# Projection weights and mixes in a scan: loads placed apart from their casts

## The chip, the cores and the metric

The kernel runs on one core of one Trainium2 chip. The metric is the time of one execution in device microseconds (us), as the median of the runs. The profile comes from one further execution on the same core, and its engines are called PE (TensorE: matmuls; PEld its weight loads), DVE (VectorE), ACT (ScalarE), POOL (GpSimd) and SP (SyncE, whose queue issues most of the DMAs here).

## What is computed

One step of a hybrid backbone with one layer. 128 context tokens and 2048 latent tokens of width 1024 pass an RMS norm, one input projection, two groups of heads, one output projection, a gated residual and a last RMS norm.

```python
def _layer(x, mod, s0, is_latent, lp):
    shift, scale, gate = jnp.split(mod, 3, axis=-1)
    h = _rmsnorm(x, lp['norm_g']) * (1.0 + scale) + shift
    proj = h @ lp['w_in']
    r, k, v, g_a, b_gate, c_gate, u_conv, g_b = jnp.split(proj, IN_SPLITS, axis=-1)
    rkv = _token_shift(jnp.concatenate([r, k, v], axis=-1), lp['shift_mu'].reshape(-1), is_latent)
    ya, s_final = _wkv(h, r, k, v, s0, lp)
    ya = ya.astype(x.dtype) * jax.nn.silu(g_a)
    yb = b_gate * _short_conv(c_gate * u_conv, lp['conv_w'], is_latent) * jax.nn.silu(g_b)
    u = jnp.concatenate([ya, yb], axis=-1) @ lp['w_out']
    return x + gate * u, s_final
```

`_wkv` is a delta-rule state update, token after token, run in both directions over eight heads of 64. Head group A (the "attention" half, 512 channels) comes from it; head group B (the "conv" half, 512 channels) comes from a short convolution and needs no scan.

## The kernel before, in words

Phase 1 (up to about 1004 us) computes the input projection, the gates and the conv half, and stores the operands of the scan and the mixed activations to scratch in HBM: `mixT` holds, for each token, the 1024 channels that enter the output projection. The conv channels of `mixT` are complete when phase 1 ends; the attention channels come out of the scan, an output block at a time.

Phase 2 is the scan, in NST = 17 stages. A round plays a string of letters (`ROUND`, `ROUND_FILL`, `ROUND_MORE`, `ROUND_END`, `ROUND_LAST`, lines 750 to 754). The loop in `main` runs round s for stage s: `L` (psF, psG), `U` and `u` (psU, psW) and `B` (psX, psE) prepare stage s+1 with matmuls, `b` is what was left of the stage's own preparation, `S` is one of the state steps (matmul psS, then DVE's `sv` on L1163), `f` and `T` finish an output block of the stages before (`finish`), and `a` is one piece of filling work from the output projection: three matmuls into psa (L1419 to L1421). Every fp32 operand is split into a high and a low half, so a product is three matmuls: high by high, high by low, low by high.

The order of PE in the scan is written out by these strings: `mm`, `tr` and `pin` chain each matmul behind the one before (`behind`, `O.last`). `now` ties another instruction behind the last matmul. What is not tied is placed by the scheduler; the order on each engine's queue is then fixed. SP issues DMAs in that order.

The output projection's weights `wout` are 1024 by 1024. Rows 512 to 1023 (k = 4 to 7, the conv half) are loaded in the first three rounds by `conv_weights` (`woraw`, L1398), cast to the high half by ACT (`split`, L1386) and reduced to the low half by DVE (L1387). Rows 0 to 511 are loaded, cast and reduced in the last rounds by `att_weights` (L1444, low half by POOL). The activations of a tile of 128 tokens are loaded by `load_mix` (L1403): `mxc` is the conv half and becomes `mhc`, `mxa` the attention half and becomes `mha`.

`fill` multiplies the conv half ahead, for the nine tiles of AHEAD: eight pieces (psa) a tile, stored as z0. In the middle rounds (`ROUND_FILL`) three pieces stand one by one, so a tile's mix is loaded every second or third round, in the same call that casts it.

POOL inverts the small triangular blocks of the stages (`solve_steps`, L951 to L971) with the scratch tiles `zt`, `ztmp` and `ab`; `partI(s + 7)` starts it seven stages ahead, with `ab` loaded on SP's queue (L941). The result goes to scratch (L971) and comes back as `zc` (L1043) when stage s+1 is prepared.

`finish(p, blk, y)` turns a block of scan outputs into attention channels of `mixT`: it loads the gate `sg` (L1201), squares y into `w` (ACT), reduces it, scales y (L1218), loads q into a second `w`, transposes with psT (L863), multiplies by gate and weight into `yo` (L1231), adds q (L1233) and stores `yo` to `mixT` (L1237). The tiles `sg`, `w` and `yo` have one buffer each.

PSUM has eight banks: in the scan `ps_tile` (L829) draws the pools p2 (three banks) and pm (one, every fourth call), psS has three and psa one.

Phase 3, the tail, finishes the projection tile by tile (psu, the order of TILES): the attention half, with the conv half too where it was not done ahead, then gate, residual, norm and store.

Of the kernel before, what the change touches and what calls it, by code (L numbers as in the profile page):

```python
# [745 lines left out]
NST = 17  # L746
# [11 lines left out]
def phase2(K):  # L758
# [45 lines left out]
    def setup_rest():  # L804
# [54 lines left out]
    def now(r):  # L859
        behind(r, O.last)  # L860
# [327 lines left out]
    def finish(p, blk, y):  # L1188

        t0 = NCTX + 512 * blk if blk is not None else 0  # L1190
        sg = tl([128, 512], "sg", 1)
# [18 lines left out]
        w = tl([128, 4, 128], "w", 1)  # L1210
        P.activation(w[:], y[:], AF.Square)
        yield
        ss = tl([128, 8], "yss", 2)
        V.tensor_reduce(ss[:], heads(w[:]), mybir.AxisListType.X, ALU.add)
# [4 lines left out]
        q = tl([128, 512], "w", 1)  # L1219
# [9 lines left out]
        o = tl([128, 512], "yo", 1)  # L1229
# [40 lines left out]
    def main():  # L1270
# [13 lines left out]
        tail = fill = iter(())  # L1284
        conv = K.conv_weights()
        for s in range(NST):
# [6 lines left out]
            for _ in range(3 if s < 3 else 0):  # L1293
                next(conv, None)
            if s == 2:
                fill = K.fill()
                next(fill)
            if NST - 4 < s < NST - 1:
                K.att_weights(s - NST + 3)
            gens = dict(L=W, b=own, u=uu, U=uu, B=bb, S=partS(s, st, sts.get(s + 1)))  # L1300

            def play(tokens):
                for c in tokens:
# [4 lines left out]
                    elif c == "T":  # L1308
                        for f in todo:
                            run(f)  # L1310
                    elif c == "a":
                        next(fill, None)
                    else:
                        next(gens[c])
                        if c == "S":
                            next(tail, None)

            if more:
                play(ROUND if s < 3 else ROUND_FILL if s < NST - 4 else ROUND_MORE if s < NST - 2 else ROUND_END)
            else:  # L1320
                for k in (2, 3):
                    K.att_weights(k)
                play(ROUND_LAST)
# [7 lines left out]
                run(fill)  # L1331
# [8 lines left out]
        for p in (O.pS, O.p2):  # L1340
            p.close()
        K.rest(tail)
        O.pf.close()
# [3 lines left out]
    K.early, K.main, K.spare, K.ahead1, K.fill_tile, K.pin, K.now = early, main, spare, ahead1, fill_tile, pin, now  # L1347
# [25 lines left out]
def phase3(K):  # L1373
# [8 lines left out]
    wk = {}  # L1382

    def split(hi, lo, raw, copy, eng):

        copy(hi, raw)  # L1386
        eng.tensor_tensor(lo, raw, hi.bitcast(F32), ALU.subtract)  # L1387
# [4 lines left out]
    def conv_weights():  # L1392
        for k in CONV:
            t = [O.r.tile([128, 1024], F32R, name=f"wo{x}{k}") for x in "hl"]
            wk[k] = [[x[:, c] for c in HALF] for x in t]
            for n, c in enumerate(HALF):
                raw = O.r.tile([128, 512], F32, tag="raw", name=f"woraw{k}", bufs=1)
                K.now(D(raw[:], A["wout"][k * 128:(k + 1) * 128, c]))  # L1398
                split(wk[k][0][n], wk[k][1][n], raw[:], P.copy, V)
                yield  # L1400

    def load_mix(raw, i, ks):
        K.now(D(raw.rearrange("p (k t) -> p k t", t=128), S["mixT"].rearrange("(k p) t -> p k t", p=128)[:, ks[0]:ks[0] + 4, i * 128:i * 128 + 128]))  # L1403

    def conv_mix(i):

        raw = O.r.tile([128, 512], F32, tag="raw", name=f"mxc{i}", bufs=1)
        load_mix(raw[:], i, CONV)
        t = O.r.tile([128, 1024], F32R, tag="mhc", name=f"mhc{i}", bufs=2)
        m = [t[:, c] for c in HALF]  # L1410
        split(*m, raw[:], P.copy, V)
        return m

    def product(ps, m, ks, h, n, start, stop, pin=lambda r: None):
# [4 lines left out]
        pin(T.matmul(ps[:], hi[:, c], wh, start=start and n == 0, stop=False))  # L1419
        pin(T.matmul(ps[:], hi[:, c], wl, start=False, stop=False))  # L1420
        pin(T.matmul(ps[:], lo[:, c], wh, start=False, stop=stop and n == 3))  # L1421

    def fill():

        nxt = conv_mix(AHEAD[0])
        yield
        for x, i in enumerate(AHEAD):
            m = nxt
            for h in range(2):
                ps = K.fill_tile(f"psa{i}_{h}")  # L1430
                for n in range(4):
                    product(ps, m, CONV, h, n, True, True, K.pin)
                    if n == 0 and h and x + 1 < len(AHEAD):
                        nxt = conv_mix(AHEAD[x + 1])
# [6 lines left out]
    def att_weights(k):  # L1441

        raw = K.spare(f"woraw{k}", F32, ("ab", "ab2")[k % 2])
        K.now(D(raw[:], A["wout"][k * 128:(k + 1) * 128, :]))  # L1444
        if k == 3:
            wk[k] = [[K.spare(f"wo{x}3{c}", F32R, "F", 512)[:] for c in range(2)] for x in "hl"]
        else:
            t = [K.spare(f"wo{x}{k}", F32R, f"o{(2, 0, 1)[k]}{n}") for n, x in enumerate("hl")]
            wk[k] = [[x[:, c] for c in HALF] for x in t]
        for n, c in enumerate(HALF):  # L1450
            split(wk[k][0][n], wk[k][1][n], raw[:, c], P.copy, G)

    def tail():
        O.pr = Pool(K, "p3pr", "right", 1, PSUM)
# [7 lines left out]
        for s in range(2):  # L1462
            D(gb[:, s], S["gate"][s:s + 1, :].broadcast_to((128, 1024)))
        fg = tl([128, 1024], "fg", "", b=1)
        D(fg[:], A["fg"].broadcast_to((128, 1024)))
        eps = tl([128, 1], "eps3", "", b=1)
        V.memset(eps[:], 1e-6)
        yield

        for i in TILES:  # L1470
            t0 = i * 128
            mc = None if i in AHEAD else conv_mix(i)
            assert K.mixed[(i - 1) // 4 if i else None] == (4 if i else 1)
            raw = K.spare(f"mxa{i}", F32, "zt", 512)
            load_mix(raw[:], i, ATT)
            t = tl([128, 1024], "mha", i, F32R)
            ma = [t[:, c] for c in HALF]
            split(*ma, raw[:], P.copy, V)
            if not mc:
                z0 = tl([128, 1024], "z0", i)  # L1480
                D(z0[:], S["z0"][i])
            xt = tl([128, 1024], "x3", i)
            D(xt[:], A["x"][t0:t0 + 128, :])
# [3 lines left out]
            last = i == TILES[-1]  # L1487
            for n, cs in enumerate(HALF):
                ps = O.pu.tile([128, 512], F32, tag="u", name=f"psu{i}_{n}")
                if mc:  # L1490
                    for k in range(4):
                        product(ps, mc, CONV, n, k, True, False)
                for k in range(4):
                    product(ps, ma, ATT, n, k, not mc, True)
                if mc:
                    V.tensor_tensor(z[:, cs], ps[:], gb[:, s, cs], ALU.mult)
                else:
                    V.tensor_tensor(z[:, cs], ps[:], z0[:, cs], ALU.add)
# [19 lines left out]
    K.weights, K.conv_weights, K.fill, K.att_weights, K.tail, K.rest = weights, conv_weights, fill, att_weights, tail, rest  # L1518
# [45 lines left out]
```

## Time and profile before

| | us |
|---|---|
| median of 3 runs | 1682.65 |
| lowest, highest | 1678.48, 6477.67 |
| the profiled execution | 1678.87 |
| its span, first to last instruction | 1677.1 |
| mean granted TensorE clock | 0.965 of full speed |

An engine's busy time is the sum of its instructions; register, semaphore and DMA-issuing instructions are not in it. A row of the timeline has its start, its length, the engine, the line, what is written and read, how many were put together, and in brackets the idle time just before and what ended it. A row for SP (SPq) is the issue of a DMA, not its transfer. The windows view gives busy times and the clock that the throttle granted to PE for chosen stretches. The waits view gives, for each engine, the total, the number and the longest of the idle times by what ended them. A wait for several things is put down to the last one.

### The profile page before, as it was taken

The numbers are of one execution on the slowest core, as the hardware profiler recorded it, in microseconds if no ns is written. First come the engines' busy times: TensorE is split into PE (matmuls) and PEld (weight loads), VectorE is DVE, ScalarE is ACT, GpSimd is POOL, SyncE is SP. The second block draws the span as 40 slices with busy tenths as digits, with TensorE's granted clock in tenths as the row PEclk, the third lists the DMA queues.
The fourth block names the chain that finished last, engine by engine and source line by source line (L and its number), as shares of the span: only waits on it lengthen the run. The fifth ranks groups of instructions, "written<-read, shape, count | busy, mean of one in ns | idle before, by whom it ended". The sixth has DMA issues, their size and how long they took to land.

```text
span 1677.1 us, 42417 instructions
## 1 busy us (share of the span) xinstructions
PE 1545.4 (92%) x17160; PEld 1402.0 (84%) x17160; DVE 1123.9 (67%) x2246; ACT 778.4 (46%) x1645; POOL 575.4 (34%) x1030
## 2 busy tenths in 40 slices
PE   5899999999999999999999996898889898887998
PEld 2799998999999999999899895777777787665886
DVE  5876877884648775568786964575566665556664
ACT  4544565553426344255443114656556565542332
POOL 0011221110112111012863656687887800101431
PEclk8999999999999999999999998799899899999999
DMA  9677767665646565656758576566575654427652
GB/s 378 202 259 242 252 240 257 221 217 203 219 136 200 210 191 180 219 177 205 244 190 281 199 228 184 148 184 167 156 221 162 174 152 146 114 84 257 232 200 101
DMA packets 242451, 336.67 MB, mean 201 GB/s; under 512 B 91784, under 2 KB 192392, under 8 KB 228176
## 3 DMA queue, kind: packets, MB, share of 16 engines
q1 hardware_dynamic: 233712, 323.27, 60.1%
q10 hardware_dynamic: 7344, 6.76, 1.3%
q0 software_dynamic: 1200, 3.93, 0.6%
q8 instruction: 135, 2.21, 0.6%
q14 instruction: 60, 0.49, 0.1%
HBM read 212.64 MB, written 121.26 MB: 199 GB/s over the span
## 4 chain that ended last, share of the span: by engine, by line
PE 44%; DVE 9%; POOL 7%; DMA 7%; ACT 4%; issue 3%; SPq 1%; DVEq 0%; ACTq 0%; POOLq 0%
PE psE L849 3%; POOL zt L966 3%; PE psu L1419 3%; PE psu L1421 3%; PE psu L1420 3%; DMA mxc<-scr_mixT 2%; POOL ztmp L963 2%; PE psS L849 2%; DMA woraw<-in_wout 1%; ACT fg L838 1%; PE mmc L166 1%; PE mmg L168 1%; PE mmg L166 1%; PE mmg L167 1%; PE psX L849 1%
## 5 line engine op out<-in xcount | busy, mean ns | idle before, releaser
L966 POOL TENSOR_TENSOR zt<-zt,ztmp 128x30 f32<-128x30 f32 (+7 forms) x390 | 155.1, 398 | 30.6
L849 PE MATMUL psE<-fg 128*64 128x128 f32 x2176 | 156.0, 290 | 0.7 <-ACT fg L838 0.7
L849 PEld LDWEIGHTS psE<-fg 128*64 128x64 f32 x2176 | 128.2, 147 | 12.3 <-ACT fg L840 5.4
L849 PE MATMUL psS<-sv,E 128*64 128x64 f32 x2176 | 101.2, 238 | 22.7 <-DVE sv L1163 20.0
L849 PEld LDWEIGHTS psS<-sv,E 128*64 128x64 f32 x2176 | 85.9, 148 | 36.5 <-DVE sv L1163 26.1
L329 POOL TENSOR_TENSOR shk<-rawl 128x384 f32<-128x384 f32 (+1 forms) x24 | 23.7, 989 | 242.7 <-ACT rawl L325 222.9
L840 ACT COPY E<-psE 128x256 f32<-128x256 f32 x136 | 50.4, 373 | 113.7 <-DVE E L1125 105.7
L1064 DVE TENSOR_TENSOR fg<-psG,consts 64x256 f32<-64x256 f32 x136 | 57.3, 421 | 61.1 <-PE psG L849 45.8
L838 ACT ACTIVATE fg<-psX 64x512 f32<-64x512 f32 x136 | 80.5, 592 | 36.2 <-PE psX L849 34.3
L963 POOL TENSOR_TENSOR ztmp<-ab,zt 128x60 f32<-128x60 f32 (+4 forms) x165 | 86.5, 524 | 12.9
L1125 DVE TENSOR_TENSOR E<-psE,consts 128x256 f32<-128x256 f32 x136 | 56.8, 418 | 46.3 <-PE psE L849 44.4
L1163 DVE TENSOR_TENSOR sv<-psS,pc 64x128 f32<-64x128 f32 x254 | 64.8, 275 | 27.7 <-PE psS L849 25.4
L1500 POOL TENSOR_TENSOR z<-z,x 128x512 f32<-128x512 f32 x32 | 45.7, 1429 | 103.8 <-DVE z L1499 56.1
L329 POOL TENSOR_TENSOR shv<-rawl 128x384 f32<-128x384 f32 (+1 forms) x24 | 20.8, 866 | 163.8 <-ACT rawl L325 162.3
L166 PE MATMUL mmc<-h,w 128*128 128x384 f32 (+1 forms) x192 | 64.9, 338 | 5.9 <-ACT q1r L327 4.1
L446 POOL COPY pcs<-pp 128x6 f32<-128x6 f32 (+1 forms) x48 | 21.2, 443 | 139.1 <-ACT pp L435 135.1
L166 PE MATMUL mmg<-h,w 128*128 128x384 f32 (+1 forms) x192 | 64.2, 334 | 3.8 <-ACT q1v L327 3.8
L840 ACT COPY fg<-psG 64x256 f32<-64x256 f32 x136 | 49.9, 367 | 33.3 <-DVE fg L1064 28.8
L166 PE MATMUL mmb<-h,w 128*128 128x384 f32 (+1 forms) x192 | 63.3, 330 | 1.5 <-ACT ta L439 1.5
L166 PE MATMUL mmgb<-h,w 128*128 128x384 f32 (+1 forms) x192 | 64.0, 333 | 0.4 <-ACT q1r L327 0.3
L167 PE MATMUL mmg<-h,w 128*128 128x384 f32 (+1 forms) x192 | 63.9, 333 | 0.0
L168 PE MATMUL mmg<-h,w 128*128 128x384 f32 (+1 forms) x192 | 63.8, 332 | 0.0
(323 smaller groups left out, 5165.1 us busy)
## 6 DMA issues: line engine op xcount, KB each, us to landing
w<-scr_wsp SPq DMA_DIRECT2D x68, 1024.0 KB, 5.8
scr_wsp<-w SPq DMA_DIRECT2D x34, 1024.0 KB, 4.9
scr_ops<-pair SPq DMA_DIRECT2D x80, 384.0 KB, 3.8
wr<-in_win SPq DMA_DIRECT2D x34, 512.0 KB, 6.0
o<-scr_ops SPq DMA_DIRECT2D x32, 512.0 KB, 4.5
fg<-scr_ops SPq DMA_DIRECT2D x120, 128.0 KB, 3.9
x<-in_x SPq DMA_DIRECT2D x17, 512.0 KB, 3.4
wadas<-in_wada SPq DMA_DIRECT2D x8, 1024.0 KB, 13.2
```

The lines of the kernel that those rows point to most:

```text
L166: T.matmul(ps[:, :n], w[:, 0, k], hh[:, 0, k, :n], start=k == 0, stop=False)
L167: T.matmul(ps[:, :n], w[:, 0, k], hh[:, 1, k, :n], start=False, stop=False)
L168: K.dense = T.matmul(ps[:, :n], w[:, 1, k], hh[:, 0, k, :n], start=False, stop=k == 7).ins
L838: P.activation(dst, src, AF.Copy, scale=-1.0)
L840: P.copy(dst, src)
L849: r = T.matmul(*a, start=True, stop=True, **k)
L963: eng.tensor_tensor(tv, ab[:, j:j + 2, j + 2:32].unsqueeze(1).broadcast_to((128, kn, 2, n)), zt[:, :kn, j:j + 2].unsqueeze(3).broadcast_to ...
L966: last = eng.tensor_tensor(zt[:, :kn, j + 2:32], zt[:, :kn, j + 2:32], tv[:, :, r], ALU.subtract).ins
L1064: V.tensor_tensor(g.gs[H[1 - h], g.op, h, us], ps[gi][r, :, 64:128], B.mG[r, g.d].unsqueeze(1).broadcast_to((64, 4, 64)), ALU.mult)
L1125: V.tensor_tensor(to(H[1]), of(H[1]), B.mE[:, g.d].unsqueeze(1).broadcast_to((128, 4, 64)), ALU.mult)
L1163: r = V.tensor_tensor(dst, sp[gi][0:64, q], B.pc[0:64, d, 2 * p:2 * p + 2, c:c + 1].broadcast_to((64, 2, 64)), ALU.mult)
L1419: pin(T.matmul(ps[:], hi[:, c], wh, start=start and n == 0, stop=False))
```

## The change

Line numbers after the change are a few higher: `mm` records as L851, `tr` as L866, `split` as L1381 and L1382, the conv weights' load as L1392, `load_mix` as L1399, the three matmuls of a piece all as L1424, the `sg` and q loads as L1206.

- New letters `c`, `m`, `w`, `x` in the rounds' strings call `conv_weights`, `mixes`, `att_weights` and `first_mixes`. Each call does one step, either a load or a cast with its low half, and both are tied behind the last matmul. ORDER gives a string for each round.
- Conv weights are loaded 128 by 1024 into the two `mhc` buffers, one letter before their casts; rounds 1 to 4 hold them, and round 0 has none. `mixes` loads a tile's mix at one `m` and casts it at the next.
- Pieces stand in twos, four in a `ROUND_FILL`, from round 5 on; rounds 0 to 4 have none. AHEAD loses tile 0, whose conv half is multiplied in the tail (24 psu matmuls more, 24 psa fewer).
- PSUM: pm gets two banks and is drawn by two calls of five, so five banks rotate; psS has two banks where it had three.
- In `finish`, the blocks 2 and 3 of p = 3 (of the last rounds) put `sg` into a place tagged "ztmp" and `w`, q and `yo` into places tagged "zt", which are POOL's solve scratch.
- The tail loads two tiles ahead, and its casts stand behind the first matmul of the tile before; three tiles' mixes are loaded before it begins; the TILES order differs.

What this does to the order of the queues, at three places. First SP's queue in the change, in round 10, from the `sg` loads on (waits in brackets: the engine or DMA queue whose semaphore is awaited):

```order
L1206 DMA sg_16579<-scr_sg 128x512 [waits DMAHW4_49,DVE_49]
L1206 DMA sg_18450<-scr_sg 128x512 [waits DMAHW5_49,Pool_49]
L1243 DMA scr_mixT<-yo_16472 128x512 [waits DMAHW6_49,DVE_49]
L1017 DMA fg_9817<-scr_ops_57 64x2x256 [waits DMAHW0_49,PE_49]
L1006 DMA sv_16594<-scr_vt 64x1024 [waits DMAHW1_49,DVE_49,PE_49]
L991 DMA sv_16594<-scr_sti 64x128 [waits DMAHW2_49]
L1006 DMA sv_16597<-scr_vt 64x1024 [waits DMAHW3_49,DVE_49,PE_49]
L991 DMA sv_16597<-scr_sti 64x128 [waits DMAHW4_49]
L1017 DMA fg_9817<-scr_ops_57 64x2x256 [waits DMAHW5_49]
L1017 DMA fg_9818<-scr_ops_58 64x2x256 [waits DMAHW6_49,PE_49]
L1206 DMA w_16588<-scr_q 128x512 [waits DMAHW7_49,DVE_49]
```

The same stretch of SP's queue before, and with it the load of the corresponding sg (sg_18503), which stood 84 rows further on, in one of the last rounds:

```order
L1201 DMA sg_16628<-scr_sg 128x512 [waits DMAHW3_49,DVE_49]
L1237 DMA scr_mixT<-yo_16524 128x512 [waits DMAHW5_49,DVE_49]
L1014 DMA fg_9817<-scr_ops_57 64x2x256 [waits DMAHW6_49,PE_49]
L1003 DMA sv_16643<-scr_vt 64x1024 [waits DMAHW7_49,DVE_49,PE_49]
L988 DMA sv_16643<-scr_sti 64x128 [waits DMAHW0_49]
L1003 DMA sv_16646<-scr_vt 64x1024 [waits DMAHW1_49,DVE_49,PE_49]
L988 DMA sv_16646<-scr_sti 64x128 [waits DMAHW2_49]
L1014 DMA fg_9817<-scr_ops_57 64x2x256 [waits DMAHW3_49]
L1014 DMA fg_9818<-scr_ops_58 64x2x256 [waits DMAHW4_49,PE_49]
L1201 DMA w_16637<-scr_q 128x512 [waits DMAHW5_49,DVE_49]
...
L1201 DMA sg_18503<-scr_sg 128x512 [waits DMAHW5_49,DVE_49]
```

What moved: the sg load of a late finish (sg_18450) stands about four rounds earlier, directly behind sg_16579, and waits for POOL; its awaited instruction is the last one of POOL's last solve. The store of yo, the fg, sv and q loads (w_16588) of rounds 11 and 12 stand behind it.

Second, ACT's order around the cast of a mix, before (zb, fg, zr and E are operands of the scan that ACT writes):

```order
L1088 ACTIVATE zb<-zc_15164,consts 128x16x32 [waits DMAHW1_49]
L1088 ACTIVATE zb<-zc_15164,consts 128x16x32
L1386 CAST mhc_15217<-mxc_15215 128x512 [waits DMAHW7_49]
L840 COPY fg_9817<-psG_0_0_15220 64x256 [waits DVE_49]
L840 COPY fg_9818<-psG_1_0_15221 64x256 [waits DVE_49]
L840 COPY zr_15246<-psU_15248 32x512 [waits PE_49]
L840 COPY zr_15246<-psU_15248 32x512
L840 COPY fg_9817<-psG_0_0_15220 64x256 [waits DVE_49]
```

and in the change:

```order
L840 ACTIVATE zb<-psW_15280 32x16x32 [waits PE_49,Activation_49]
L840 ACTIVATE zb<-psW_15280 32x16x32
L1381 CAST mhc_15363<-mxc_14851 128x512
L842 COPY E_15246<-psE_0_11_15327 128x4x64 [waits DVE_49]
L842 COPY y_15343<-psS_0_0_15227 64x512 [waits DVE_49]
L842 COPY y_15350<-psS_1_0_15233 64x512 [waits DVE_49]
L842 COPY E_15268<-psE_1_11_15352 128x4x64 [waits DVE_49]
```

What moved: the cast waited for its own load (a DMA queue's semaphore), which stands in the same round; now the load (mxc_14851) is a round older, another wait has covered it, and the cast has none of its own.

Third, ACT's order around a cast of conv weights, before, in round 0:

```order
L1386 CAST woh_11171<-woraw_11173 128x512 [waits DMAHW4_49]
L838 ACTIVATE fg_9817<-psX_0_1_11220 64x2x256 [waits PE_49]
L1088 ACTIVATE zb<-zc_11195,consts 128x16x32
L1088 ACTIVATE zb<-zc_11195,consts 128x16x32 [waits Activation_49]
L1386 CAST woh_11171<-woraw_11177 128x512 [waits DMAHW2_49]
L840 COPY fg_9817<-psG_0_0_11242 64x256 [waits DVE_49]
L840 COPY fg_9818<-psG_1_0_11243 64x256 [waits DVE_49]
```

and in the change, in round 1:

```order
L842 COPY E_11738<-psE_1_10_11739 128x4x64 [waits DVE_49,Activation_49]
L1381 CAST woh_11582<-woraw_11584 128x512 [waits DMAHW2_49]
L840 ACTIVATE zb<-psW_11750 32x16x32 [waits PE_49,Activation_49]
L840 ACTIVATE zb<-psW_11750 32x16x32
L842 COPY E_11716<-psE_0_11_11799 128x4x64 [waits DVE_49]
L842 COPY y_11815<-psS_0_0_11704 64x512 [waits DVE_49]
L842 COPY y_11822<-psS_1_0_11710 64x512 [waits DVE_49]
L842 COPY E_11738<-psE_1_11_11824 128x4x64 [waits DVE_49]
L840 ACTIVATE fg_9817<-psX_0_0_11861 64x2x256 [waits PE_49]
```

What moved: the casts stand in other rounds, one in a place, and each still waits on the semaphore of its load, which is now issued at the letter c before it, ten or eleven letters of the string ahead.

The diff, cut to what the prediction speaks of:

```diff
-ROUND_FILL = "f L b a L u U S a b S b U S b S b L a B L T S a B S B S B S B".split()
-ROUND_MORE = "f L b a a L u U S a b S a b U S b S b L a B a L T S a B S a B S B S B".split()
-ROUND_END = "f L b a a L u U S a b S b U S b b S L a B L a a a a T S B S B S B S B B".split()
-ROUND_LAST = "a S b a S b a S b a S b a".split()
+ROUND_W = "c f L b L u U S b S b U c S b S b L B L T S B S B c S B S B".split()
+ROUND_M = "c f L b L u U S b S b U c S b S b L B L T S B S B c S B S B m".split()
+ROUND_FILL = "f L b L u U S a a b S b U S b S b m L B L T S a a B S B S B S B".split()
+ROUND_MORE = "m f L b a L u U S a a b S b U S a b S b L a B L m T S a a B S a B S B S B".split()
+ROUND_ATT = "w m f L b a L u U S a a b S b U w S a b S b L a B L m T S a a B S a B S B S B".split()
+ROUND_END = "w m f L b a L u U S a a b S b U w S b b S L B L m a a a a T w S a B S B S B w S B B".split()
+ROUND_LAST = "a a S w b S a x b S w a b x S a b x".split()
+ORDER = [ROUND] + [ROUND_W] * 2 + [ROUND_M] * 2 + [ROUND_FILL] * 8 + [ROUND_MORE, ROUND_ATT, ROUND_END, ROUND_LAST]
...
-        O.pm.close()
-        O.pf = Pool(K, "p2f", "right", 1, PSUM)
-        O.pm = Pool(K, "p2n", "right", 1, PSUM)
         O.p2 = Pool(K, "p2s", "left", 3, PSUM)
-        O.pS = Pool(K, "p2S", "left", 3, PSUM)
+        O.pS = Pool(K, "p2S", "left", 2, PSUM)
+        O.pf = Pool(K, "p2f", "left", 1, PSUM)
...
-        if O.pm is not None and (O.n % 4 == 0 or O.p2 is None):
+        if O.pm is not None and (O.n % 5 < 2 or O.p2 is None):
...
-        sg = tl([128, 512], "sg", 1)
+        other = p == 3 and blk in (2, 3)
+        place = lambda tag: spare(f"{tag}{K.u()}", F32, "ztmp" if tag == "sg" else "zt", 512) if other else tl([128, 512], tag, 1)
+        sg = place("sg")
...
-        w = tl([128, 4, 128], "w", 1)
+        w = place("w")
...
-        q = tl([128, 512], "w", 1)
+        q = place("w")
...
-        o = tl([128, 512], "yo", 1)
+        o = place("yo")
...
+        side = dict(a=K.fill(), c=K.conv_weights(), m=K.mixes(), w=K.att_weights(), x=K.first_mixes())
...
-    AHEAD = [5, 6, 7, 8, 9, 10, 11, 12, 0]
-    TILES = [5, 6, 7, 13, 8, 14, 9, 15, 10, 16, 11, 1, 12, 2, 0, 3, 4]
+    AHEAD = [5, 6, 7, 8, 9, 10, 11, 12]
+    TILES = [5, 6, 7, 0, 8, 13, 9, 14, 10, 15, 11, 16, 12, 1, 2, 3, 4]
...
+            raw = O.r.tile([128, 1024], F32, tag="mhc", name=f"woraw{k}", bufs=2)
+            K.now(D(raw[:], A["wout"][k * 128:(k + 1) * 128, :]))
+            yield
             for n, c in enumerate(HALF):
-                raw = O.r.tile([128, 512], F32, tag="raw", name=f"woraw{k}", bufs=1)
-                K.now(D(raw[:], A["wout"][k * 128:(k + 1) * 128, c]))
-                split(wk[k][0][n], wk[k][1][n], raw[:], P.copy, V)
+                split(wk[k][0][n], wk[k][1][n], raw[:, c], V)
                 yield
...
+    def mixes():
+        for i in AHEAD:
+            K.now(conv_raw(i))
+            yield
+            conv_split(i)
+            yield
...
+    def first_mixes():
+        K.now(att_raw(TILES[0]))
+        yield
+        K.now(att_raw(TILES[1]))
+        yield
+        att_split(TILES[0])
...
+            if q + 2 < len(TILES):
+                loads(q + 2)
+                if n == 0 and not last:
+                    j, f = TILES[q + 1], O.first
+                    at = lambda K, r: K.behind(r, f)
+                    att_split(j, at)
+                    if j not in AHEAD:
+                        conv_split(j, at)
```

More of the change, by code (lines that the diff above doesn't have):

```diff
@@ L859, in now @@
     def now(r):
-        behind(r, O.last)
+        if O.line:
+            behind(r, O.last)
     def tr(*a):
@@ L1292, in main @@
             todo = [pend.pop(0) for _ in range(len(pend) if s > NST - 4 else min(1, len(pend)))]
[L1293 to L1300, printed above, removed]
+            gens = dict(side, L=W, b=own, u=uu, U=uu, B=bb, S=partS(s, st, sts.get(s + 1)))
             def play(tokens):
@@ L1330, in main @@
                 play("SaSaSaS")
-                run(fill)
+                for k in "cmaxw":
+                    assert next(side[k], None) is None and not list(side[k])
                 O.line = False
@@ L1431, in fill @@
                 for n in range(4):
[L1432 to L1434 removed]
+                    product(ps, cm[i], CONV, h, n, True, True, K.pin)
                     if n == 3:
```

142 lines of the change are left out of this document (80 added, 62 removed).

## The prediction, made before the changed kernel ran

> **What bounds the kernel now.** I read the page first: which engine is busy, and what the chain that ended last is made of.
>
> ```profile
> span 1677.1 us, 42417 instructions
> PE 1545.4 (92%) x17160; PEld 1402.0 (84%) x17160; DVE 1123.9 (67%) x2246; ACT 778.4 (46%) x1645; POOL 575.4 (34%) x1030
> PE 44%; DVE 9%; POOL 7%; DMA 7%; ACT 4%; issue 3%; SPq 1%; DVEq 0%; ACTq 0%; POOLq 0%
> ```
>
> TensorE (PE) is the bound, 92% busy. Only its idle time, and work done at a lowered clock, can be won. POOL, busy 34% of the span, still holds 7% of the chain. Next come the stretches of scan and tail by windows (columns: length, then the busy time of PE, PEld, DVE, ACT and POOL, the granted clock, DMA share, GB/s).
>
> ```profile
> 1004.50:1357.90 353.40, 306.55 (x7005) 263.75 (x7003) 205.66 (x513) 204.74 (x423) 264.10 (x580) 0.91 0.63 174
> 1394.80:1466.80 72.00, 60.88 (x1214) 49.10 (x1210) 38.30 (x92) 38.91 (x80) 6.19 (x12) 0.93 0.40 110
> 1466.80:1546.80 80.00, 62.33 (x843) 49.21 (x839) 47.33 (x103) 30.29 (x66) 9.32 (x7) 0.94 0.50 166
> 1546.80:1669.50 122.70, 122.67 (x528) 99.02 (x528) 72.25 (x110) 36.78 (x94) 41.82 (x29) 1.00 0.55 187
> ```
>
> Length less PE busy is idle time; busy time times (1 - clock) is what the clock costs. Up to 1357.9 us that gives 46.9 us idle and 306.55 x 0.09 = 27.6 us of clock; from 1394.8 to 1466.8, 11.1 and 4.3; from 1466.8 to 1546.8, 17.7 and 3.7. The last 122.7 us are solid. These 111.3 us are about all that a change of waits can win.
>
> Who ends the idle time, by PE's waits between 1004.5 and 1669.5 us (total, times, longest):
>
> ```profile
> PE psS L849 <- DVE sv L1163: 20.0, 20, 3.2
> PE psT L863 <- DVE y L1218: 12.3, 3, 6.0
> PE psX L849 <- ACT E L840: 11.0, 10, 3.5
> PE psT L863 <- ACT fg L838: 10.2, 12, 3.9
> PE psG L849 <- DVE F L1057: 9.7, 4, 6.6
> ```
>
> The engine named is not the cause. Two places from the timeline, a weight and a mix:
>
> ```profile
> 1050.82 0.62 ACT L1386 CAST woh<-woraw 128x512 fp32r<-128x512 f32 x1 [5.55 <-DMA woraw<-in_wout]
> 1053.05 0.69 PE L849 MATMUL psG<-fg,o 64*64 64x128 f32 x4 [6.64 <-DVE F L1057]
> 1192.50 0.59 SPq L1403 DMA_DIRECT2D mxc<-scr_mixT  x1
> 1197.71 0.62 ACT L1386 CAST mhc<-mxc 128x512 fp32r<-128x512 f32 x1 [3.14 <-DMA mxc<-scr_mixT]
> 1198.37 0.69 DVE L1387 TENSOR_TENSOR mhc<-mxc,mhc 128x512 fp32r<-128x512 f32 x1 [4.45 <-ACT mhc L1386]
> 1199.63 0.69 PE L849 MATMUL psS<-sv,E 128*64 128x64 f32 x8 [2.97 <-DVE sv L1163]
> 1199.60:1209.00 9.40, 9.29 (x156) 8.71 (x158) 4.01 (x12) 3.72 (x9) 7.91 (x20) 0.51 0.23 42
> ```
>
> A load is issued and its cast stands directly in ACT's order; ACT waits for the DMA, DVE for ACT's high half, and the scan's own DVE step stands behind. PE then idles 6.64 or 2.97 us. After the 2.97 us it runs the next 9.4 us at 0.51 of the clock, 9.29 x 0.49 = 4.5 us more. So this mix load, 5.2 us from issue to cast, costs the scan 7.5 us.
>
> Here a page differs. The Trainium skill, "TensorE: Matmul & The Clock Gate", Part 1, has the clock halve after an idle window of about 3.4 us and come back after about 3.4 us of work. The 2.97 us gap above lost the clock already, and the half clock lasted 9 us, so the rows decide. By the page, as an estimate, the short gaps would lose no clock and a mix load would cost 3 us.
>
> **The change, part by part.**
>
> *Loads apart from casts.* The loads that stopped ACT (conv weights, then one mix for every second round) are now issued about a round before their casts. A round that meets none is the price without the stall:
>
> ```profile
> 1226.40:1252.40 26.00, 24.66 (x596) 20.88 (x592) 18.14 (x44) 15.62 (x34) 22.40 (x48) 1.00 0.69 198
> ```
>
> It keeps 1.3 us of idle time (bank and transpose waits). 1357.9 us is about where round 11 (rounds from 0) finishes an output block: its transpose psT and DVE's use of it. Up to there I leave 10 us of the 46.9 + 27.6 = 74.5: 64.5 are won, and PE could stand there at 1357.9 - 64.5 = 1293.4 us. The price of the casts, 0.62 and 0.69 us, is unchanged; a round of 26 us covers the 5.2 us of a load; with that cover gone the stall is back at its old price.
>
> *POOL.* Now the part on which the forecast turns. In the new order of the SP queue the load of sg_18450 (output gate of a finish of the last rounds) stands in round 10. Its place is now "ztmp", the scratch of POOL's solves, and it waits for POOL's very last solve. SP issues in order, as a wait of before shows:
>
> ```profile
> 983.96 0.55 SPq L587 DMA_DIRECT2D scr_mixT<-ob  x1
> SPq L898 <- POOL zt L966: 6.7, 1, 6.7
> 990.97 0.38 SPq L898 DMA_DIRECT2D o<-scr_ops  x1
> ```
>
> Nothing left SP between 983.96 and 990.97 us while it waited for POOL. Behind sg_18450 stand in after: the store of yo, fg loads, the sv loads of stage 12, and w_16588, the q term that DVE adds in round 11. When is the last solve done? POOL's starts and end:
>
> ```profile
> 1014.73 0.20 POOL L955 COPY dgp<-ab 128x16 f32<-128x16 f32 x1 [21.78 <-DMA ab<-scr_at]
> 1109.12 0.20 POOL L955 COPY dgp<-ab 128x16 f32<-128x16 f32 x1
> 1136.73 0.20 POOL L955 COPY dgp<-ab 128x16 f32<-128x16 f32 x1
> 1343.25 0.61 POOL L971 DMA_DIRECT2D scr_zt<-zt  x1 [0.30 <-POOL zt L966]
> POOL dgp L955 <- DMA ab<-scr_at: 37.1, 4, 21.8
> POOL dgp L955 <- DMA a<-scr_lo: 7.0, 1, 7.0
> ```
>
> Eleven solves lie between 1014.73 and 1343.25 us; one takes 27.61 us back to back. Of the 328.5 us, 37.1 - 21.8 + 7.0 = 22.3 were waits for loads, which come earlier once the rounds are shorter. The first start is set before any place that changes. So the last solve ends at 1343.25 - 22.3 = 1321 us (bounds: 1014.73 + 11 x 27.61 = 1318.4 with no loss, 1343.3 if every wait stays). PE has shortened; POOL has not.
>
> Then SP must issue sg, the store, three fg, four sv pieces and w. The same queue before, the use of w, and the landing time of w's loads:
>
> ```profile
> 1333.23 0.33 SPq L1237 DMA_DIRECT2D scr_mixT<-yo  x1
> 1340.41 0.54 SPq L1201 DMA_DIRECT2D w<-scr_q  x1
> 1358.55 0.67 DVE L1233 TENSOR_TENSOR yo<-yo,w 128x512 f32<-128x512 f32 x1
> DMA to landing us min/median/max: 3.0/3.0/3.0
> ```
>
> From the store to the end of w's issue it is 7.7 us there, some waits among it. The bounds are 0.33 + 0.54 us, the two issues alone, and 7.7; as most of those loads stand in it too, I take 5.5. With the landing of 3.0 and 1.5 us for DVE's add and what it holds up, PE goes on at 1321 + 10 = 1331 us. PE, which could be there at 1293.4, stands 38 us. Of the 64.5 us won only 1357.9 - 1331 = 26.9 remain. After such a gap PE starts at half clock: 4.5 us more, as above.
>
> *Behind that place* before takes 1677.1 - 1357.9 = 319.2 us. Removed: in the two rounds from 1394.8 to 1466.8, 11.1 us idle and 4.3 of clock, from late mix and attention-weight loads; I keep 1.4: -14.0. The finishes of the last rounds had one place "w" for both, and shared waits stand here:
>
> ```profile
> 1488.69 0.66 PE L863 MATMUL psT<-consts,y 128*128 128x128 f32 x2 [4.75 <-DVE y L1218]
> 1523.37 0.90 PE L863 MATMUL psT<-consts,y 128*128 128x128 f32 x3 [6.02 <-DVE y L1218]
> ```
>
> Own places remove the first (-4.8). In the new order 19 tail matmuls of 122.7/528 = 0.232 us, 4.4 us, stand ahead of the second: -4.4 and about -2 of clock.
>
> *Pieces.* One piece alone and two together:
>
> ```profile
> 1356.84 0.50 PE L1419 MATMUL psa<-woh,mhc 128*128 128x512 f32 x1
> 1357.73 0.33 PE L849 MATMUL psE<-fg 128*64 128x128 f32 x2
> 1425.62 0.50 PE L1419 MATMUL psa<-woh,mhc 128*128 128x512 f32 x1
> 1427.22 0.99 PE L849 MATMUL psG<-fg,o 64*64 64x128 f32 x28
> ```
>
> Alone 0.89 us, a pair 1.60: -0.18 a pair, 12 to 15 pairs here, -2.5. Tile 0's eight pieces leave the scan (8 x 0.89 = -7.1) and come back as 24 tail matmuls (+5.6): -1.5.
>
> *Added waits.* The state product psS has two banks where it had three; the trace has no such wait. Bounds: nothing, or in each round one wait for ACT's copy, 1.1 us like the mean of psX's (11.0 in 10 waits above); the kernel's scan has kept PE busy for 24.66 of 26 us with waits of that kind, so near the lower: +1. Five rotating banks may take back part of the 11.0 us of psX; I take nothing. The loads for two tail tiles ahead fall together at the tail's start (DMA share 0.50 around it now): 0 to 5 us, +3.
>
> Sum behind the place: -14.0 - 4.8 - 6.4 - 2.5 - 1.5 + 1 + 3 + 4.5 = -20.7, so 298.5 us. Span 1331 + 298.5 = 1629.5 us. The profiled execution took 1678.87 us for its span of 1677.1, 1.8 more: 1631 us. The median shown, 1682.65, is 0.2% above that execution; I add nothing.
>
> **The rivals.**
>
> *The wait on POOL does not bite.* If sg_18450 goes out before its need blocks anything, or what stands behind it is not needed that early, PE goes on from 1293.4, without 4.5 us of clock: 1293.4 + 294.0 + 1.8 = 1589 us. For it: the trace of before has no sg load that waits for POOL. Against it: the order has that wait, and the 983.96 row shows what SP does with one. Chance 0.15.
>
> *The gain is lost to other waits.* If POOL keeps its 22.3 us of waits (last solve at 1343.3) and the tail's burst and two psS banks cost their upper ends (5 us and 13 x 1.1 = 14 us, where I took 4), the sum is 1631 + 22 + 15 = 1668 us; with four fifths of that loss 1661, within 2%. For it: ab loads too wait for an older solve, and SP for them. Chance 0.11.
>
> *SP never regains its lead: slower.* Before, w was issued at 1340.41 for a use at 1358.55, 18 us ahead; after the stop nothing is ahead. If every one of the six rounds behind waits for its loads again, each with the 10 us from above and 4.5 us of half clock, that is 6 x 14.5 = 87 us: 1718 us, slower than before; from four rounds on (1689) it decides. Against it: the 7.7 us from store to w hold most of what is blocked, and a round has 26, so SP should recover in about two rounds. Chance 0.04.
>
> *The change does not do what it says* (casts still meet their loads): the POOL wait would then hardly be felt, since PE came late anyway, and the time stays near 1680. Against it: in the new order ACT's casts of mixes stand a round behind their loads. Chance 0.03.
>
> **How the numbers follow.** Forecast 1631 us, chance 0.67; the other four 0.15, 0.11, 0.04, 0.03. The range reaches to the free case below (1589, with 3 for its own error: 1586) and to the lost-gain case above, 1662; it leaves out some 0.17. About 2%, 34 us, is what a measurement of this kernel tells from no change: below 1649 is faster. The forecast lies 18 us inside and gives 0.67 less 0.02 for its own tail, the free case 0.15, and the lost-gain case 0.03 where it loses less: 0.83. Slower by over 2% (above 1716) takes the never-recovered case but a quarter, 0.03. The same: 0.14.
>
> **What would show it.** Right: PE without 6 us gaps and with the clock near 1 from round 1 to 10; one gap of 30 to 45 us on PE in round 11, ended by DVE's yo or sv; SP waiting over 40 us for POOL at the sg load (L1206); POOL's last solve ending between 1318 and 1330 us; ACT's casts (L1381) with no wait for a DMA; no 6 us gap before the last psT. Wrong: no long SP wait for POOL and a span near 1587; a gap behind round 11 in every round; casts that still wait for mxc; or a scan held by psS for ACT's copies of y.

## The result, and the profile after

The changed kernel took 1655.26 us (median of 4 runs, 1654.05 to 1659.12) against 1683.99 for the kernel before; the ratio is 0.9844, 95% interval 0.9812 to 0.9876. The four runs before hold one of 6477.67 us; without it their median is 1682.65, so the gain is 27 to 29 us. That lies inside the range, but it is little more than half of the 52 us that were forecast, and by the prediction's own line (faster below 1649 us) it counts as the same, to which it gave 0.14. The interval leaves no doubt that there is a gain; it is a small one. The profiled execution is the longest of the four, 1659.12 us with a span of 1657.3.

The forecast's central claim was one long stop. First SP's waits in the changed kernel (total, times, longest), then SP's issues and POOL's first start and last end around it:

```profile
SPq L1206 <- POOL zt L969: 38.1, 1, 38.1
1287.80 0.51 SPq L1206 DMA_DIRECT2D sg<-scr_sg  x1
1326.53 0.33 SPq L1206 DMA_DIRECT2D sg<-scr_sg  x1
1326.96 0.38 SPq L1243 DMA_DIRECT2D scr_mixT<-yo  x1
1332.36 0.54 SPq L1206 DMA_DIRECT2D w<-scr_q  x1
1018.88 0.20 POOL L958 COPY dgp<-ab 128x16 f32<-128x16 f32 x1 [23.88 <-DMA ab<-scr_at]
1326.80 0.61 POOL L974 DMA_DIRECT2D scr_zt<-zt  x1 [0.30 <-POOL zt L969]
```

SP issued nothing for 38.1 us, until POOL's last solve was done at 1326.5. The eleven solves took 307.9 us, 28.0 each: POOL ran back to back, as it had not before. The Trainium skill, "DMA: Bandwidth & Descriptors", section "Anatomy of one DMA — SWDGE (gpsimd) path", says that a DMA's wait for a semaphore happens on the issuing sequencer, not in the DMA engines. The 38.1 us on SP's queue agree, and so does everything that stood still behind.

What stood still is seen on DVE and PE:

```profile
1330.34 0.75 DVE L1237 SCALAR_TENSOR_TENSOR yo<-psT,gwh,sg 128x512 f32<-128x512 f32 x1 [18.16 <-DMA scr_mixT<-yo]
1337.71 0.69 DVE L1239 TENSOR_TENSOR yo<-yo,w 128x512 f32<-128x512 f32 x1 [5.33 <-DMA w<-scr_q]
1331.66 1.47 PE L851 MATMUL psS<-sv,E 128*64 128x64 f32 x16 [16.41 <-DVE sv L1166]
1340.03 1.12 PE L851 MATMUL psS<-sv,E 128*64 128x64 f32 x16 [5.20 <-DVE sv L1166]
1345.92 0.69 PE L851 MATMUL psS<-sv,E 128*64 128x64 f32 x16 [3.06 <-DVE sv L1166]
```

The first thing missed is not the q load w, as I had it, but the store of yo: yo has one buffer, so DVE's next yo waits for its store, and the scan's sv stands behind on DVE. Then w is late, then the scalings of the next finish. PE says "sv" three times, 24.7 us in all. Now the stretches (columns as before):

```profile
1298.50:1315.20 16.70, 16.66 (x402) 14.23 (x400) 9.00 (x23) 10.67 (x22) 14.48 (x33) 1.00 0.06 20
1315.20:1351.80 36.60, 11.85 (x194) 10.31 (x192) 9.60 (x22) 4.37 (x11) 10.18 (x24) 0.63 0.62 167
1351.80:1378.30 26.50, 24.91 (x599) 21.49 (x595) 16.61 (x43) 19.50 (x40) 0.00 (x0) 1.00 0.63 170
1438.30:1649.30 211.00, 196.62 (x1395) 158.52 (x1393) 123.39 (x210) 68.73 (x163) 54.08 (x38) 0.94 0.50 168
```

Round 11 runs from 1298.5 to 1351.8, 53.3 us; the round behind it takes 26.5. While SP stands, from 1298.5 to 1315.2 us, the core's DMA share is 0.06: next to nothing is being loaded. The last row, from round 15 to PE's end, is set against the same stretch of the kernel before:

```profile
1466.80:1669.50 202.70, 185.00 (x1370) 148.22 (x1366) 119.58 (x212) 67.07 (x159) 51.14 (x36) 0.97 0.53 178
```

It has become 8.3 us longer where I had counted 11 us less. PE's waits from 1438 us on, in the changed kernel:

```profile
PE psa L1424 <- ACT z L1437: 4.7, 1, 4.7
PE psS L851 <- DVE so L1166: 4.4, 2, 3.6
PE psT L866 <- DVE y L1224: 3.7, 2, 1.9
PE psu L1424 <- DVE yo L1237: 1.1, 1, 1.1
```

and in the kernel before, from 1466 us to PE's end:

```profile
PE psT L863 <- DVE y L1218: 12.3, 3, 6.0
PE psS L849 <- DVE so L1163: 2.0, 3, 0.8
PE psu L1419 <- DVE z L1498: 1.6, 1, 1.6
```

The wait of psT for y has shrunk from 12.3 to 3.7 us; a wait of psa for ACT is new, and that of psS for so has doubled. The casts behave as forecast: none of the eight casts of conv mixes ahead of the tail (mhc) has a wait for its load, for example

```profile
1280.78 0.62 ACT L1381 CAST mhc<-mxc 128x512 fp32r<-128x512 f32 x1
```

### The profile page after: what moved, and what is told of

It reads as the page before. It is cut to its first block, busy times and chain, and to the rows that moved or that the text cites. A ratio compares the mean times of both kernels' runs of the same rounds, so it can differ in the third digit from the quotient of the medians.

```text
span 1657.3 us, 42441 instructions
## 1 busy us (share of the span) xinstructions
PE 1529.5 (92%) x17160; PEld 1398.4 (84%) x17160; DVE 1123.2 (68%) x2244; ACT 774.8 (47%) x1643; POOL 580.0 (35%) x1030
## 5 line engine op out<-in xcount | busy, mean ns | idle before, releaser
L851 PE MATMUL psE<-fg 128*64 128x128 f32 x2176 | 152.0, 285 | 0.1
L851 PE MATMUL psS<-sv,E 128*64 128x64 f32 x2176 | 99.1, 232 | 54.8 <-DVE sv L1166 36.6
L851 PEld LDWEIGHTS psS<-sv,E 128*64 128x64 f32 x2176 | 83.1, 142 | 70.2 <-DVE sv L1166 43.4
L851 PEld LDWEIGHTS psE<-fg 128*64 128x64 f32 x2176 | 124.4, 143 | 10.9 <-issue 4.9
L1424 PE MATMUL psu<-woh,mha 128*128 128x512 f32 x272 | 89.2, 396 | 0.0
L166 PE MATMUL mmc<-h,w 128*128 128x384 f32 (+1 forms) x192 | 65.0, 339 | 5.9 <-ACT q1r L327 4.1
L166 PE MATMUL mmg<-h,w 128*128 128x384 f32 (+1 forms) x192 | 64.2, 334 | 3.8 <-ACT q1v L327 3.8
L1543 ACT ACTIVATE x<-z 128x512 f32<-128x512 f32 x34 | 21.5, 632 | 91.7 <-POOL z L1542 83.2
L167 PE MATMUL mmc<-h,w 128*128 128x384 f32 (+1 forms) x192 | 64.3, 335 | 0.0
```

The costliest lines, as they stand in the source:

```text
L166: T.matmul(ps[:, :n], w[:, 0, k], hh[:, 0, k, :n], start=k == 0, stop=False)
L167: T.matmul(ps[:, :n], w[:, 0, k], hh[:, 1, k, :n], start=False, stop=False)
L851: r = T.matmul(*a, start=True, stop=True, **k)
L1424: r = T.matmul(ps[:], l[:, c], r, start=start and n == x == 0, stop=stop and n == 3 and x == 2)
```

## The experiments

Each is timed against the kernel before on its own chip; ratios to it compare across the groups better than medians.

**The gate load tied to its round.** The changed kernel, with one load held where it is used:

```diff
-                D(t_[:], S[nm][p * 128:(p + 1) * 128, t0:t0 + 512])
+                r = D(t_[:], S[nm][p * 128:(p + 1) * 128, t0:t0 + 512])
+                if other and nm == "sg":
+                    now(r)
```

> The changed kernel, but the gate load of the two late finishes is tied behind the matmul of its own round, so that it can no longer be moved up to round 10; its place is still POOL's scratch. Theory (SP stands 38 us for POOL's last solve behind that load, and round 11 takes 53.3 us where its neighbours take 26): round 11 falls to 26 us and nothing takes its place: 1655 - 27 = 1628 us, 1622 to 1636. Rival (the scan is held at that place by POOL or by late loads in any case): 1645 us or more, with a wait of another load for POOL in round 11 or 12.

Measured: 1623.01 us, ratio 0.9668 (0.9617 to 0.9719), 30 us under the changed kernel by the ratios, 32 by the medians. Rounds 10 and 11, now 25.9 and 24.3 us:

```profile
1266.20:1292.10 25.90, 24.12 (x596) 21.07 (x592) 19.22 (x47) 14.88 (x33) 22.41 (x50) 1.00 0.71 203
1292.10:1316.40 24.30, 24.23 (x597) 21.04 (x593) 18.69 (x46) 15.54 (x33) 21.13 (x46) 1.00 0.77 209
```

PE idles 0.1 us in round 11. POOL's last solve ended at 1324.7, after that round, and no load of a finish waited for it: a single load's place in the queue cost about as much as the whole change had won.

**The place alone.** The same kernel without the tie, but with the gate in its old place:

```diff
-        sg = place("sg")
+        sg = tl([128, 512], "sg", 1)
```

> The changed kernel with one line undone: the gate of the late finishes has the place 'sg' again, shared with the other finishes, and no tie; w, q and yo stay in POOL's scratch. Theory (the place alone makes the load wait for POOL, and the load alone holds SP): as with the tied load, 1623 us, 1620 to 1627. Rival (w, q and yo in POOL's scratch hold DVE or ACT too, the gate load is only the first): 1635 us or more.

Measured: 1627.7 us, ratio 0.9682 (0.9638 to 0.9726), just above the range expected and the same as with the tie within the intervals. So it is the gate's place in POOL's scratch together with the early position; that w, q and yo there hold anybody is not seen, within some 7 us.

**The same places in the kernel before.** Only the diff's lines on `other`, `place`, sg, w, q and yo are taken over, the first of them

```diff
-        sg = tl([128, 512], "sg", 1)
+        other = p == 3 and blk in (2, 3)
+        place = lambda tag: spare(f"{tag}{K.u()}", F32, "ztmp" if tag == "sg" else "zt", 512) if other else tl([128, 512], tag, 1)
+        sg = place("sg")
```

> The kernel before, with only the places of the late finishes in POOL's scratch. In its queue too the gate load moves up to round 10 and waits for POOL's last solve, but there the scan comes 40 us later. Theory (the cost is the distance between the scan and POOL): SP stands about 12 us, from 1331 to 1343, the loads behind are needed from 1356 on, so PE loses 0 to 6 us and wins 4.7 from the own places: 1678 to 1686 us. Rival (the wait itself, or the places, cost 20 us or more wherever they stand): 1700 us or more.

Measured: 1682.33 us, ratio 1.0016 (0.9989 to 1.0043): no difference clear of the noise. SP does stop there too, shorter, and PE still meets it, through an fg load that comes late:

```profile
SPq L1203 <- POOL zt L966: 14.8, 1, 14.8
1361.38 0.63 ACT L1214 ACTIVATE w<-y 128x512 f32<-128x512 f32 x1 [3.86 <-DMA fg<-scr_ops]
1363.50 0.45 PE L849 MATMUL psS<-sv,E 128*64 128x64 f32 x8 [3.40 <-DVE sv L1163]
```

The stop is not free here. In the profiled execution rounds 11 and 12 take 30.0 and 32.1 us where they took 26.0 and 26.4, some 10 us. The rest wins a part of it back: psT waits for y no more (12.3 us before), though psu now waits 9.4 us for ACT and DVE. So a stop of 14.8 us cost some 10 us where the scan comes late, and one of 38.1 us some 30 where it comes early. The cost goes with the distance between scan and POOL, which the rest of the change had opened.

**Stalls ahead of the stop.** Two edits put loads back directly ahead of their casts, each on the changed kernel and on the one with the tie. For the conv weights:

```diff
-            K.now(D(raw[:], A["wout"][k * 128:(k + 1) * 128, :]))
             yield
+            K.now(D(raw[:], A["wout"][k * 128:(k + 1) * 128, :]))
             for n, c in enumerate(HALF):
```

> The changed kernel, but each load of the conv weights stands directly ahead of its first cast again (rounds 1 to 4). Theory (PE reaches round 11's block at 1315 us and is let go at 1331 whatever it did before): four stalls of some 7 us in rounds 1 to 4 are taken up by the 16 us that PE stands there, so no more than 0 to 14 us are lost: 1655 to 1669 us, and POOL's last solve still ends near 1327 us. Rival (the stop at POOL is no common bound, stalls add up): 1655 + 28 = 1683 us.

> Both edits: the gate load tied to its round and the conv weights' loads directly ahead of their casts. Theory: without the stop at POOL the four stalls count in full, 20 to 30 us above the kernel with the tied load alone (1648 to 1658 us if that has 1628). Rival (stalls in these rounds are hidden in any case, or the stop at POOL did not hide them): the same difference as between the kernel with merged conv loads and the changed kernel, within 4 us.

Measured: 1654.55 us (ratio 0.9863, 0.9813 to 0.9913) and 1624.4 (0.9675, 0.9629 to 0.9721). Neither differs from its kernel without the edit. The first was expected by the theory too, but the second refutes the reason: these loads cost nothing that can be measured directly ahead of their casts. In the tied kernel with this edit one cast of eight waited for its load:

```profile
1043.77 0.62 ACT L1383 CAST woh<-woraw 128x512 fp32r<-128x512 f32 x1 [2.33 <-DMA woraw<-in_wout]
1065.32 0.62 ACT L1383 CAST woh<-woraw 128x512 fp32r<-128x512 f32 x1
```

SP issued each load 5 to 7 us ahead of its cast (1038.11 us for the first). So this pair could not test what the stop hides, and it shows that the separate letter was not what freed rounds 0 to 2. What remains of the change there is two buffers of double width instead of one, one load a round instead of three halves, and later rounds; which of these did it was not tried.

For the mixes (in the kernel before too a middle round holds four pieces, not three, so a tile's mix is loaded every second round):

```diff
         for i in AHEAD:
-            K.now(conv_raw(i))
             yield
+            K.now(conv_raw(i))
             conv_split(i)
             yield
```

> The kernel with the tied gate load, and each mix loaded directly ahead of its cast again. Theory (a mix load at its cast costs the scan 5 to 7.5 us, idle and clock, as in the kernel before): eight of them, 1623 + 40 to 1623 + 60 us. Rival (it was the single buffer and the place in the order, not the missing round, that stalled the kernel before; SP runs far enough ahead): 1623 to 1630 us. By the page's rule that a gap under 3.4 us leaves the clock alone it would be some 3 us a mix, 1647 us, as an estimate.

> The changed kernel (gate load moved up as it was), but each mix is loaded directly ahead of its cast again, every second round from round 4. Theory (a stop at POOL until 1331 us swallows what came before): of four merged mixes ahead of round 11 at 5 to 7.5 us each, 16 us are hidden, and the four behind count: 1655 + 8 to 1655 + 45, and at least 10 us less above the changed kernel than the same edit costs the kernel with the tied load. Rival (SP issues these loads as far ahead as it did the conv weights', so nothing is lost): 1653 to 1658 us.

Measured: 1652.83 us with the tie (ratio 0.9818, 0.9797 to 0.984) and 1662.86 without (0.9879, 0.9855 to 0.9904). Against their kernels that is 0.0150 x 1682 = 25 us with the tie and 0.0035 x 1682 = 6 us without, each uncertain by 7 to 9 us from the intervals. The stop swallows some 19 us, and SP's wait says the same: it fell from 38.1 to

```profile
SPq L1206 <- POOL zt L969: 18.2, 1, 18.2
```

POOL's last end stayed, 1324.2. This is the test that the conv weights could not give, and the theory stands, by SP's wait more firmly than by the times: until round 11 only POOL counted. The size of a mix was wrong, though: 25 us for eight is 3 us each. Six of the eight casts waited, 2.1 to 4.8 us. One of them, with what it did to PE, in the tied kernel with merged mixes:

```profile
1185.21 0.62 ACT L1383 CAST mhc<-mxc 128x512 fp32r<-128x512 f32 x1 [4.51 <-DMA mxc<-scr_mixT]
1186.15 0.58 PE L851 MATMUL psG<-fg,o 64*64 64x128 f32 x4 [3.08 <-ACT E L842]
1186.20:1195.50 9.30, 8.22 (x94) 6.42 (x96) 5.95 (x13) 4.34 (x9) 7.97 (x18) 0.63 0.51 175
```

3.08 us idle and 8.22 x 0.37 = 3.0 us of clock: 6 us for this one, near the 7.5 that I had read from one row, which was a bad one of its kind. The rule of the Trainium skill, "TensorE: Matmul & The Clock Gate", Part 1, gave a total close to the measured one (1647 as an estimate, by 3 us a mix), but not for its reason: this gap too was under 3.4 us and cost the clock.

**The last rounds.** On the kernel with the tie, one piece of round 15 is moved ahead of L:

```diff
-... w S b b S L B L m a a a a T w S a B ...
+... w S b b S a L B L m a a a T w S a B ...
```

> The kernel with the tied gate load; in round 15 one of the four pieces that stand together goes ahead of the round's L, so that the half of a tile that ends there is copied out of psa's one bank before the next half begins. Theory (the missing gain behind round 11 is new waits in the last rounds; the 4.7 us wait of psa for ACT's copy z is one of them, with 3 to 4 us of lowered clock behind it): 1623 - 8 = 1615 us, 1613 to 1619. Rival (PE is held there by the scan's chain anyway, the wait moves to psF or psS): 1621 to 1625 us.

Measured: 1617.18 us, ratio 0.9608 (0.9585 to 0.9631). Again on another chip, beside the last experiment:

> The kernel with the tied gate load and the spread pieces again, beside the one without the places on the same chip: 1617 us, 1614 to 1621.

1618.77 us, ratio 0.9634 (0.9612 to 0.9657). The psa wait is gone. PE's waits from 1404 us on:

```profile
PE psS L851 <- DVE so L1166: 3.9, 3, 2.9
PE psT L866 <- DVE y L1226: 3.7, 2, 1.9
PE psu L1426 <- DVE yo L1239: 1.4, 1, 1.4
```

From round 15 to PE's end it now takes 202.2 us instead of 210.0 with the tied load alone (211.0 in the changed kernel): 4.7 us of wait and the clock that stood behind it. The ratios give 6 to 10 us, with an interval as wide.

**The final states.** Three places instead of two, and, on the spread kernel, their stores issued by ACT:

```diff
-                        so = tl([64, 2, 64], "so", 2)
+                        so = tl([64, 2, 64], "so", 3)
```

```diff
-                        D(S["nst"][:, d, 2 * p:2 * p + 2, :], so[:])
+                        P.dma_start(S["nst"][:, d, 2 * p:2 * p + 2, :], so[:])
```

> The kernel with the tied gate load and three places instead of two for the final states (so) on their way out. Theory (psS waits 5.6 us for DVE's so, which waits for the store of the one two before, 3.9 us of it in one piece and with half a clock behind it): one more place takes 2 to 3 us of the waits and a part of the clock: 1623 - 4 = 1619 us, 1616 to 1621. Rival (the stores are held on SP's queue behind the loads of the last rounds, so a place more helps nothing): 1622 to 1624 us.

> The kernel with the tied gate load and the spread pieces; the stores of the final states (so) are issued by ACT instead of SP. Theory A (a store of so takes some 5 us from issue to landing whoever issues it, and eight come within 5 us of work for two places): the wait of psS for so stays at 3 to 6 us, 1617 us, 1615 to 1619. Theory B (the stores stand behind yo's store, the gate loads and the mixes on SP): the wait falls under 2 us, with its lowered clock, 1610 to 1613 us.

Measured: 1627.89 us (ratio 0.9665, 0.9635 to 0.9694; with two places 0.9668) and 1621.7 (0.9651, 0.9616 to 0.9687; from SP 0.9608 and 0.9634). Neither helps. With three places DVE only meets its wait one state later, as long as before; from ACT's queue the wait is as long as from SP's, 7.7 us in all against 7.0:

```profile
1446.07 0.28 DVE L1166 TENSOR_TENSOR so<-psS,pc 64x128 f32<-64x128 f32 x1 [4.25 <-DMA out_nst<-so]
DVE so L1166 <- DMA out_nst<-so: 7.7, 6, 3.0
```

(the first row from the kernel with three places, the second from that with ACT's stores). In the former the first store was issued at 1440.70 and its place came free at 1446.07: 5.4 us, and the states follow each other faster than that. From ACT a place came free 1.9 to 4.4 us after its store's issue, so not 5 us whoever issues, but still later than the next state. More places were not tried, so the cure is open.

**The late finishes' places.** The spread kernel with all finishes in single places (`other = False`):

> The kernel with the spread pieces, with all finishes in the single places sg, w and yo as in the kernel before, so that nothing of them lies in POOL's scratch. Theory (my term for the own places was right: the single place w made two finishes of one round wait for each other, 4.8 us before): 1617 + 5 to 1617 + 10 us, with a wait of psT for y of 4 us or more. Rival (the tail's matmuls and the spread hide that wait, the places were not needed): 1615 to 1619 us.

Measured: 1626.93 us, ratio 0.9695 (0.968 to 0.971), 8 us above the spread kernel beside it by the medians, 10 by the ratios. The wait is there in full:

```profile
PE psT L866 <- DVE y L1226: 15.1, 2, 10.0
```

So the places are worth 8 us or more in this kernel, where I gave them 4.8. They are a gain in themselves; their price came from the one load that moved up with them.

## Why the prediction was half right

**Right: the stop and its end.** The last solve was put at 1321 us (measured 1326.5, in an execution whose first solve began 4.2 us later), PE's return at 1331 (1331.66), and SP's wait over 40 us (38.1, just under). That the place makes the load wait, that SP holds what stands behind it, and that POOL then sets the time, the tied load, the gate's own place, the kernel before with the places and the merged mixes all show. That PE's return came out to within 1 us is luck, though. The last solve ended 5.5 us later than I said (4.2 of them from the start), and PE was let go 5.1 us behind it, by the store of yo, where I had 10 us, for w. The w path itself was right: DVE's add began at 1337.71, 11.2 us behind the solve, but by then PE had returned and stood again.

**Wrong without effect: the arrival.** PE was to reach the place at 1293.4 us and stand 38; it came at 1315.2 and stood 16.4. The 64.5 us that I had taken as won there were 42.7. Rounds 1 to 4 took 28.0, 24.0, 25.5 and 31.1 us, with gaps of 2.9 and 3.2 us that I had not foreseen (last section). I had left 10 us of idle time and clock up to there; from 1004.5 to 1315.2 us PE idled 29.0 us, and the clock cost 281.66 x 0.03 = 8.4. The round from which I read 1.3 us of idle time holds four pieces, while rounds 1 to 4 hold none and idle 16.9 us together; how much of it pieces would fill was not tried. POOL would have swallowed the difference anyway. But it makes the rival's time wrong: without the stop I gave 1589 us, and the tied load measured 1623. In its profiled execution, 33 us longer than the rival's span, 15 us lie ahead of the place, which PE reached at 1308.8, and 18 behind it.

**Wrong, and the step that failed: the sum behind the place.** I wrote -20.7 us, 298.5 instead of 319.2; from PE's return to the end it took 1657.3 - 1331.7 = 325.6. Four small terms (-2.5, -1.5, +1 and +3) add up to nothing and are left out. Of the 27.1 us that are missing:

- 5 us in round 11 itself. I had 4.5 us of half clock and no second wait. After the store, w and the next finish were late as well: 5.20 and 3.06 us, at 0.63 of the clock over the stretch. SP made up its lead in the same round (the next one takes 26.5), which speaks against the rival in which it never does.
- 2 us in rounds 12 to 14. They fell from 26.4 + 34.5 + 37.5 to 26.5 + 29.5 + 30.5 us, 11.9 of the 14.0 that I had.
- 20 us from round 15 on: +8.7 to the end of the span, where my terms gave -11.2. Idle time there fell from 17.7 to 14.4 us only; the clock cost 196.62 x 0.06 = 11.8 us where it had cost 185.00 x 0.03 = 5.6; and the work at full clock grew by 184.8 - 179.5 = 5.3 us (the clock's two digits leave these last two uncertain by 1 to 2 us). The work fits tile 0, though no run put it back: PE has 1395 matmuls in the stretch where it had 1370. I booked the 24 tail matmuls (+5.6) against eight pieces leaving the same stretch (-7.1), but rounds 15 and 16 hold 16 pieces before and after; the pieces that left were those of earlier rounds, and what that won there the stop at POOL swallowed. The psa wait is a cost of the change that I did not see at all: I priced a pair of pieces by PE's time, and four in a row by nothing, though a half of a tile now ends behind the first of them and psa has one bank. (Before, four stood in a row as well, but the half ended one piece ahead of them, with psX and psG between.) Spreading them shortened the stretch by 7.8 us. The wait for so doubled, which I took as unchanged; what would cure it is open.

The single term that was too small on the other side is the places (4.8 for 8 or more). The bank terms (+1 for psS, nothing for psX) show in the waits view alone: psS waited 4.9 us for ACT's copy of y, in three places, psX no longer for ACT. No run separated them.

**The best version** is the changed kernel with the tied gate load and the spread pieces: 1617.18 and 1618.77 us, ratios 0.9608 and 0.9634, 35 to 40 us under the changed kernel.

## What to carry to other kernels

A buffer shared with a slow engine is a wait in the queue of whoever fills it: when a load gets a place in another engine's scratch, look up where the scheduler puts that load, and tie it to the round that uses it. When one path is shortened, list what ran beside it with slack (POOL's solves here): whatever waits for that work at a fixed place becomes the bound, and further gains ahead of it are swallowed. And a term counts only in the stretch in which the work lies: work that moves from a covered stretch to one where PE is solid is a loss, however small it looks in the sum.

## What the runs showed of the hardware that was not expected

PE stood for nothing that the profile shows ("issue") in the changed kernel and in its variants. At psS in the changed kernel these are 8.3 us in five waits, four of them in rounds 1 to 6, for example

```profile
1047.72 1.01 PE L851 MATMUL psS<-sv,E 128*64 128x64 f32 x14 [2.92 <-issue]
1122.70:1132.00 9.30, 9.29 (x152) 8.68 (x156) 2.96 (x8) 3.60 (x7) 8.01 (x22) 0.52 0.33 71
```

The second row is the clock behind another of them, of 3.16 us at 1122.71: 0.52 for 9.3 us, 4.5 us more. Such gaps stand at like places in the variants (0.2 to 4.9 us at psS) and had no like in the kernel before, nor in the one before with the new places. What PE waits for there no run told apart; it stays open.

A gap of about 3 us cost clock on top, whatever its cause: after gaps of 2.6 to 4.7 us the stretches of 9 us behind ran at 0.50 to 0.82 of full speed in the kernels here, 1.7 to 4.6 us each.
